# First weights in runs of 1, 1, 2 and 4 tiles, squares of the input placed after its splits and summed by VectorE, and seven products of zeros at the start

## The chip, the cores and the metric

The kernel runs on one core of a Trainium2 chip. The metric is the device time of one execution in microseconds (us), median of several runs; lower is better. Five engines share the work: TensorE (PE; its weight loads are listed as PEld), VectorE (DVE), ScalarE (ACT), GpSimd (POOL) and SyncE (SP), whose queue issues nearly all DMA transfers here.

## The reference, cut to what matters

The model is a two-layer trunk on 512 tokens with 16 meta tokens put in front (528 tokens, width 1024): a forgetting attention with 16 heads, a gated MLP with a causal convolution, an HGRN2 recurrence, and another gated MLP. Only the attention's beginning is touched by the change:

```python
def rms_norm(x, gain):
    x32 = x.astype(jnp.float32)
    y = x32 * lax.rsqrt(jnp.mean(x32 * x32, axis=-1, keepdims=True) + EPS)
    return (y * gain.astype(jnp.float32)).astype(x.dtype)

def fox_attention(h, norm_g, w_in, b_f, q_gain, k_gain, w_out):
    xn = rms_norm(h, norm_g)
    q, k, v, f_logit, o_gate = jnp.split(xn @ w_in, [D, 2 * D, 3 * D, 3 * D + H], axis=-1)
    q = rms_norm(q.reshape(B, L, H, hd), q_gain).astype(jnp.float32) * (hd ** -0.5)
    k = rms_norm(k.reshape(B, L, H, hd), k_gain).astype(jnp.float32)
    ...
    s = jnp.einsum('bqhd,bkhd->bhqk', q_blk, k) + c_blk[..., None] - c[:, :, None, :]
```

The mean of the squares over the 1024 features of a token is only needed as a factor per token, so projections can start on the unscaled input, and the factor can come later.

## The kernel before, in words

The input lies transposed: 8 blocks (`h[:, kt, :]`) of 128 features by 528 tokens. Every float32 product is made from three products of rounded parts: `normsplit` (L269) makes `xhi` on ScalarE (L273) and the remainder `xlo` on VectorE (L274) for each of the 8 blocks, and `weights` (L174) does the same with a weight tile: a DMA into `raw`, a cast `hi` on ScalarE, a subtraction `lo` on VectorE (L122). `proj_unit` (L196) then runs hi by hi (L204), hi by lo of the input (L207) and lo by hi of the input (L208) for each block, 24 products for one half of the tokens (264) and 128 output features.

Heads are worked in 8 pairs. A pair's q and k are projected (`stage_a`), for the first pair block by block in the order in which blocks arrive; the two result banks `p` are shared by all projections, and a bank comes free when ScalarE has read it twice: a square `sqq` (L486) and a scaled copy `rawq` or `rawk` (L487). A pair then goes through this chain:

- the squares are summed per head (L495), copied (`strow`) and carried by 4 DMAs (L500) into `am`; VectorE takes the inverse root in ten small steps (L284 to L288), giving `yr`; 2 DMAs (L510) carry it into `rows`;
- `stage_n`: four products with a selection matrix (L524, here called the spreading products) lay the factors over a bank `d`, one bank for all four; VectorE multiplies `rawq` and `rawk` by it (L525), and the result, split into `stg`, is carried by 6 DMAs (L551) into the slots `pk` of the pair's two heads; the forget terms `cneg` follow by DMA (L560);
- `stage_l`: per head six groups of scores (L666 to L669), maxima on VectorE (L679 to L687), exponentials with sums on ScalarE (L115), a logarithm, and then one small product (L700) that turns the result into rows, which DMAs (L705, L706) carry into the head's slot;
- `stage_t`: the scores once more with that row in (L722, L723) and the products with v (L737).

The mean of squares of the input itself is a chain of its own: `sumsq` (L259) squares each block on ScalarE (L263, L266) and adds it on GpSimd (L267); a product per token tile (L296) finishes the sum; its inverse root scales v and the gates, and through 4 DMAs (`et`, L375) it enters the `am` step of every pair.

The order within each engine is not written by hand. The code yields pieces of work that `weave` interleaves by cost, and a scheduler then places all instructions of the program by its own model of time. Each engine, and SP's queue, runs its list in order; an instruction whose operand is late holds up everything behind it on its engine. In the first microseconds SP issues vec (228 columns of vectors), the first q and k weights in two halves each, the 8 input blocks and the constants.

Of the kernel before, what the change touches and what calls it, by code (L numbers as in the profile page):

```python
# [24 lines left out]
T = 528  # L25
NM = 16
HF = 16
NPAIR = 8
NEARLY = 4
FF = 2816  # L30
NF = FF // P
EPS = 1e-6
# [48 lines left out]
class Builder:  # L81
# [42 lines left out]
    def setup(self):  # L124
        nc = self.nc
        cp = self.cp = self.pool("const")
        self.h = cp.tile([P, KT, T], F32, name="h")
        self.vec = cp.tile([P, V_END], F32, name="vec")
        nc.sync.dma_start(self.vec, self.a["vec"])
        self.wraw = self.pool("wraw", 2)  # L130
        self.whi = self.pool("whi", 3)
        self.wlo = self.pool("wlo", 3)
        q, k = (self.weights(self.a["wqk"][0, i], KT, parts=2) for i in range(2))
        order = [(q, 0), 0, (k, 0), 1, 2, 3, (q, 1), (k, 1), 4, 5, 6, 7]
        for x in order:
            if isinstance(x, int):
                nc.sync.dma_start(self.h[:, x, :], self.a["h0"][:, x, :])
            else:
                x[0][3][x[1]]()
        self.first = q[:3], k[:3]  # L140
        cst = cp.tile([P, C_END], F32, name="cst")
        self.cst = cst
        nc.sync.dma_start(cst, self.a["cst"])
        self.ident = cst[:, C_ID : C_ID + P]
        self.identr = cp.tile([P, P], F32R, name="identr")
        nc.vector.tensor_copy(self.identr, self.ident)
        self.xhi = cp.tile([P, KT, T], F32R, name="xhi")
        self.xlo = cp.tile([P, KT, T], F32R, name="xlo")
        self.x = [(self.xhi[:, k, :], self.xlo[:, k, :]) for k in range(KT)]
        self.rsb = cp.tile([P, T], F32, name="rsb")  # L150
        self.onesd = cp.tile([P, 2], F32, name="onesd")
        nc.vector.memset(self.onesd, 1.0 / D)
        self.tiny = self.pool("tiny", 2)
        self.sqp = self.pool("sqp", 2)
        self.ps = self.pool("ps", 1, PSUM)
        self.nbank = 0
        self.ss = None

    def anybank(self):
        self.nbank += 1  # L160
# [10 lines left out]
    def vcol(self, i):  # L171
        return self.vec[:, i : i + 1]

    def weights(self, src, n, w=P, parts=1):  # L174
# [12 lines left out]
        u = hi.rearrange("p (k c) -> p k c", c=w), lo.rearrange("p (k c) -> p k c", c=w), n  # L187
        if parts == 1:
            nc.sync.dma_start(raw, src)
            nc.scalar.copy(hi, raw)  # L190
            self.sub(lo, raw, hi.bitcast(F32))
            return u
        m = n * w // parts
        return *u, [partial(load, slice(i * m, i * m + m)) for i in range(parts)]

    def proj_unit(self, ps, units, x, t0, tn, prev=None):  # L196

# [58 lines left out]
                    yield 0.66  # L256
            put(t, ps[:tn, :256])

    def sumsq(self, kt, t0=0, eng=None, pool=None):  # L259
        nc = self.nc  # L260
        if kt == 0:
            self.ss = self.sqp.tile([P, T], F32, name="ss", tag="ss", bufs=1)
            nc.scalar.square(self.ss[:, t0:], self.h[:, kt, t0:])  # L263
        else:
            sq = (pool or self.sqp).tile([P, T], F32, name="sq", tag="sq" if pool is None else "rows")
            nc.scalar.square(sq[:, t0:], self.h[:, kt, t0:])  # L266
            self.ss_last = (eng or nc.vector).tensor_tensor(self.ss[:, t0:], self.ss[:, t0:], sq[:, t0:], ALU.add)  # L267

    def normsplit(self, gcol, t0=0):  # L269
        nc = self.nc  # L270
        for kt in range(KT):
            g = self.vcol(gcol + kt)
            nc.scalar.activation(self.xhi[:, kt, t0:], self.h[:, kt, t0:], AF.Copy, scale=g)  # L273
            nc.vector.scalar_tensor_tensor(  # L274
                self.xlo[:, kt, t0:], self.h[:, kt, t0:], g, self.xhi[:, kt, t0:].bitcast(F32), ALU.mult, ALU.subtract
            )
# [45 lines left out]
    def fox(self, ctx):  # L322
        nc, tc, a = self.nc, self.tc, self.a
# [3 lines left out]
        s2 = self.pool("fox2", 2, ctx=ctx)  # L327
# [1 line left out]
        gate = self.h  # L329
        self.normsplit(V_FOXN)  # L330
        for kt in range(KT):
            self.sumsq(kt, 0, nc.gpsimd, s2)
        lone = self.lone(sp, V_FOXN, T - 32)
        identb = sp.tile([P, P], BF16, name="identb")
        maskq = sp.tile([P, P], BF16, name="maskq")
# [29 lines left out]
        start = partial(self.bank, "s")  # L365
# [7 lines left out]
        for g in range(4):  # L373
            t0, tn = full[g % 2]
# [14 lines left out]
        z, e, w, u, lf = (sp.tile([P, CW], F32, name=n) for n in ("z", "e", "w", "u", "lf"))  # L389
# [218 lines left out]
        for p in range(-3, NPAIR):  # L608
# [26 lines left out]
            while gated and p >= max(gated[0], 5 + gated[0] // 4):  # L635
                m = gated.pop(0)
# [537 lines left out]
```

## Time and profile before

| what | value |
|---|---|
| time, median of 3 runs | 1498.43 us (1496.72 to 1500.53) |
| profiled execution, its own time | 1497.61 us |
| its span | 1495.8 us |
| PE busy | 1474.4 us (99%) |
| DVE, ACT, POOL busy | 892.8, 524.9, 32.3 us |
| mean granted TensorE clock | 0.998 |
| PE idle before the first product | 6.45 us |

The span is counted from the first instruction; the profiled execution's own time is 1.8 us longer than its span and 0.8 us below the median of the runs. In a row of the timeline the first number is the start, the second the duration, then engine, line, operation, operands and shapes; brackets give idle time before it and what ended it. A row that shows several instructions merged (x2, x4) gives the time from the first start to the last end. Line numbers such as L204 are those of the kernel before.

### The profile page before, as it was taken

How to read it: one execution, taken by the hardware profiler on the slowest of the kernel's cores; microseconds unless marked ns; L12 is line 12 of the kernel's file. 1: busy time of each engine (PE TensorE's matmuls, PEld its weight loads, DVE VectorE, ACT ScalarE, POOL GpSimd, SP SyncE). 2: the span in 40 equal slices, each digit the busy share in tenths (PEclk: the TensorE clock that was granted, in tenths of full speed). 3: DMA queues.
4: the chain of work that ended last, by engine and by line, in shares of the span. 5: the costliest groups of instructions: out<-in, count | busy, mean ns of one | idle time of the engine just before them, and what ended most of it. 6: DMA issues, size and time to landing. Idle time of an engine off the chain costs nothing.

```text
span 1495.8 us, 27540 instructions
## 1 busy us (share of the span) xinstructions
PE 1474.4 (99%) x11352; PEld 1361.8 (91%) x11352; DVE 892.8 (60%) x1881; ACT 524.9 (35%) x1007; POOL 32.3 (2%) x113
## 2 busy tenths in 40 slices
PE   7999999999999999999999999999999999999999
PEld 6888888979999999999999989999999989988887
DVE  6555555775677667643335667676566667675221
ACT  5456555654233222222222333333342232222121
POOL 6000000000000000000000000000000000000000
PEclk9999999999999999999999999999999999999999
DMA  4433344413232322322322211211132232332331
GB/s 156 117 103 88 102 106 127 116 52 96 96 99 85 96 88 88 95 78 80 104 83 71 72 35 52 71 63 52 57 101 97 86 99 87 96 98 83 121 104 60
DMA packets 44821, 133.33 MB, mean 89 GB/s; under 512 B 7432, under 2 KB 7944, under 8 KB 44696
## 3 DMA queue, kind: packets, MB, share of 16 engines
q1 hardware_dynamic: 44696, 131.57, 29.1%
q8 instruction: 89, 1.46, 0.4%
q14 instruction: 36, 0.29, 0.1%
HBM read 116.10 MB, written 2.10 MB: 79 GB/s over the span
## 4 chain that ended last, share of the span: by engine, by line
PE 96%; DMA 2%; DVE 1%; SPq 1%; ACT 1%; issue 0%; DVEq 0%; ACTq 0%
PE pss L208 13%; PE pss L207 13%; PE pss L204 13%; PE psp L204 12%; PE psp L207 12%; PE psp L208 12%; PE psp L253 5%; PE psc L737 2%; PE pss L888 1%; PE pss L666 1%; PE pss L722 1%; PE pss L867 1%; PE pss L723 1%; DMA h<-h 1%; PE pss L963 1%; PE pss L894 1%
## 5 line engine op out<-in xcount | busy, mean ns | idle before, releaser
L190 ACT CAST hi<-raw 128x1024 fp32r<-128x1024 f32 (+2 forms) x218 | 221.8, 1018 | 569.4 <-PE pss L207 235.3
L122 DVE TENSOR_TENSOR lo<-raw,hi 128x1024 fp32r<-128x1024 f32 (+2 forms) x222 | 262.8, 1185 | 148.7 <-ACT hi L190 143.5
L204 PE MATMUL psp<-xhi,hi 128*128 128x264 f32 (+2 forms) x1160 | 332.9, 288 | 6.5 <-ACT xhi L273 6.5
L207 PE MATMUL psp<-xlo,hi 128*128 128x264 f32 (+2 forms) x1160 | 333.6, 288 | 3.4 <-DVE xlo L274 3.4
L208 PE MATMUL psp<-xhi,lo 128*128 128x264 f32 (+2 forms) x1160 | 332.7, 287 | 0.0
L208 PE MATMUL pss<-xhi,lo 128*128 128x264 f32 (+2 forms) x824 | 253.7, 308 | 0.0
L207 PE MATMUL pss<-xlo,hi 128*128 128x264 f32 (+2 forms) x824 | 253.0, 307 | 0.0
L204 PE MATMUL pss<-xhi,hi 128*128 128x264 f32 (+2 forms) x824 | 252.9, 307 | 0.0
L204 PEld LDWEIGHTS psp<-xhi,hi 128*128 128x128 f32 x1160 | 219.1, 189 | 11.1 <-ACT xhi L273 6.5
L207 PEld LDWEIGHTS psp<-xlo,hi 128*128 128x128 f32 x1160 | 219.5, 189 | 7.7 <-DVE xlo L274 4.1
L208 PEld LDWEIGHTS psp<-xhi,lo 128*128 128x128 f32 x1160 | 219.5, 189 | 1.2 <-issue 1.0
L204 PEld LDWEIGHTS pss<-xhi,hi 128*128 128x128 f32 x824 | 155.2, 188 | 7.8
L207 PEld LDWEIGHTS pss<-xlo,hi 128*128 128x128 f32 x824 | 155.0, 188 | 7.9
L208 PEld LDWEIGHTS pss<-xhi,lo 128*128 128x128 f32 x824 | 155.0, 188 | 7.7
L207 PE MATMUL pss<-alo,hi 128*128 128x264 f32 (+1 forms) x330 | 106.1, 322 | 0.0
L208 PE MATMUL pss<-ahi,lo 128*128 128x264 f32 (+1 forms) x330 | 106.0, 321 | 0.0
L204 PE MATMUL pss<-ahi,hi 128*128 128x264 f32 (+1 forms) x330 | 105.9, 321 | 0.0
L115 ACT ACTIVATE s<-t 128x528 f32<-128x528 f32 (+1 forms) x44 | 28.1, 639 | 121.6 <-DVE t L1056 121.6
L253 PE MATMUL psp<-hi,xhi 128*128 128x256 f32 x232 | 67.4, 290 | 2.7 <-ACT v L540 2.7
L208 PEld LDWEIGHTS pss<-ahi,lo 128*128 128x128 f32 x330 | 62.3, 189 | 4.9
L204 PEld LDWEIGHTS pss<-ahi,hi 128*128 128x128 f32 x330 | 62.1, 188 | 4.9
L253 PE MATMUL psp<-lo,xhi 128*128 128x256 f32 x232 | 66.5, 287 | 0.0
(405 smaller groups left out, 2603.3 us busy)
## 6 DMA issues: line engine op xcount, KB each, us to landing
raw<-gu SPq DMA_DIRECT2D x88, 512.0 KB
raw<-dn SPq DMA_DIRECT2D x32, 448.0 KB
pk<-stg SPq DMA_DIRECT2D x48, 264.0 KB
raw<-dn SPq DMA_DIRECT2D x16, 512.0 KB
raw<-wqk SPq DMA_DIRECT2D x14, 512.0 KB
raw<-wv SPq DMA_DIRECT2D x8, 512.0 KB
raw<-wg SPq DMA_DIRECT2D x8, 512.0 KB
raw<-hv SPq DMA_DIRECT2D x8, 512.0 KB
```

Of the source, the lines that this page charges most:

```text
L115: ins = self.nc.scalar.activation(out, in_, func, **kw)
L122: self.nc.vector.tensor_tensor(out, x, y, ALU.subtract)
L190: nc.scalar.copy(hi, raw)
L204: ins = mm(ps, hi[:, i, :], xh, start=k == 0, stop=False)
L207: mm(ps, hi[:, i, :], xl, start=False, stop=False)
L208: mm(ps, lo[:, i, :], xh, start=False, stop=k == total - 1)
L253: mm(ps[:tn, :256], y[:, t0 : t0 + tn], w, start=n == 0, stop=n == 23)
L666: mm(o, q1[0:66, qs : qs + qn], k1[0:66, c0:c1], start=True, stop=False)
L722: self.score = mm(o, k1[0:98, ks : ks + kn], q1[0:98, q0:o1], start=True, stop=False)
L723: mm(o, k2[:, ks : ks + kn], q2[:, q0:o1], start=False, stop=True)
L737: ins = mm(o, v[:kn, j, 2 * (p % 2) + hd, :], w[hd][0], start=j == 0, stop=j == last)
L867: mm(pl[:, i, :, :], kp[:, t0 : t0 + tn], qk[:, t0 // 2 : (t0 + tn) // 2, :], start=True, stop=True)
```

## The change

Five edits in `setup`, `weights`, `sumsq`, `normsplit` and `fox`:

1. The first q and k weight tiles (8 column groups of 128 each) are loaded, cast and subtracted in runs of 1, 1, 2 and 4 groups instead of two runs of 4; the DMA order is interleaved anew with the input blocks, and `vec` is issued second instead of first.
2. `warm`: VectorE sets 128 by 512 bf16 zeros, and PE multiplies them seven times into bank `d`, which nobody reads.
3. The eight squares of the input may not be placed ahead of the last `xhi` (an ordering for the scheduler, not a wait).
4. The seven additions of squares move from GpSimd to VectorE.
5. The pools for PSUM banks and for squares are opened earlier, since `warm` uses both.

```diff
+NWARM = 7
...
-        nc.sync.dma_start(self.vec, self.a["vec"])
...
+        self.warm()
-        q, k = (self.weights(self.a["wqk"][0, i], KT, parts=2) for i in range(2))
-        order = [(q, 0), 0, (k, 0), 1, 2, 3, (q, 1), (k, 1), 4, 5, 6, 7]
+        q, k = (self.weights(self.a["wqk"][0, i], KT, parts=(1, 1, 2, 4)) for i in range(2))
+        order = [(q, 0), "vec", 0, (k, 0), (q, 1), 1, (k, 1), (q, 2), 2, (k, 2), 3, (q, 3), 4, (k, 3), 5, 6, 7]
         for x in order:
-            if isinstance(x, int):
+            if x == "vec":
+                nc.sync.dma_start(self.vec, self.a["vec"])
+            elif isinstance(x, int):
                 nc.sync.dma_start(self.h[:, x, :], self.a["h0"][:, x, :])
...
+    def warm(self):
+
+        nc = self.nc
+        z = self.sqp.tile([P, T], F32, name="zero", tag="sq")[:, :256].bitcast(BF16)
+        nc.vector.memset(z, 0.0)
+        o = self.bank("d")
+        for _ in range(NWARM):
+            nc.tensor.matmul(o, z[:, :P], z, start=True, stop=True)
...
-        m = n * w // parts
-        return *u, [partial(load, slice(i * m, i * m + m)) for i in range(parts)]
+        ends = [sum(parts[: i + 1]) * w for i in range(len(parts))]
+        return *u, [partial(load, slice(e - i * w, e)) for i, e in zip(parts, ends)]
...
-    def sumsq(self, kt, t0=0, eng=None, pool=None):
+    def sumsq(self, kt, t0=0, pool=None, prev=None):
         nc = self.nc
         if kt == 0:
             self.ss = self.sqp.tile([P, T], F32, name="ss", tag="ss", bufs=1)
-            nc.scalar.square(self.ss[:, t0:], self.h[:, kt, t0:])
+            ins = nc.scalar.square(self.ss[:, t0:], self.h[:, kt, t0:])
         else:
             sq = (pool or self.sqp).tile([P, T], F32, name="sq", tag="sq" if pool is None else "rows")
-            nc.scalar.square(sq[:, t0:], self.h[:, kt, t0:])
-            self.ss_last = (eng or nc.vector).tensor_tensor(self.ss[:, t0:], self.ss[:, t0:], sq[:, t0:], ALU.add)
+            ins = nc.scalar.square(sq[:, t0:], self.h[:, kt, t0:])
+            self.ss_last = nc.vector.tensor_tensor(self.ss[:, t0:], self.ss[:, t0:], sq[:, t0:], ALU.add)
+        if prev is not None:
+            self.after(ins, prev)
...
-            nc.scalar.activation(self.xhi[:, kt, t0:], self.h[:, kt, t0:], AF.Copy, scale=g)
+            self.split = nc.scalar.activation(self.xhi[:, kt, t0:], self.h[:, kt, t0:], AF.Copy, scale=g)
...
-            self.sumsq(kt, 0, nc.gpsimd, s2)
+            self.sumsq(kt, 0, s2, self.split)
```

The scheduler places the whole attention anew from this start on, so rows far behind the edits move too. Line numbers of the changed kernel run some 14 higher in the attention (L714 is the line that was L700, L736 was L722, L680 was L666, L538 was L524). Three places follow.

The first is ScalarE's list at the very start, before:

```order
2 L183 CAST hi<-raw 128x512
3 L273 ACTIVATE xhi<-h,vec 128x528
4 L263 ACTIVATE ss<-h 128x528
5 L183 CAST hi<-raw 128x512
6 L273 ACTIVATE xhi<-h,vec 128x528
7 L266 ACTIVATE sq<-h 128x528
8 L273 ACTIVATE xhi<-h,vec 128x528
```

and now, from the end of the splits:

```order
13 L195 CAST hi<-raw 128x512
14 L287 ACTIVATE xhi<-h,vec 128x528 x3
15 L275 ACTIVATE ss<-h 128x528
16 L278 ACTIVATE sq<-h 128x528 x2
17 L202 CAST hi<-raw 128x1024
18 L278 ACTIVATE sq<-h 128x528
19 L500 ACTIVATE sqq<-psp 128x264
20 L501 ACTIVATE rawq<-psp,qg 128x264
```

The squares left their places between the splits; all eight now stand behind the last `xhi`, some of them between the reads of the first pair's result banks.

The second is PE's list where the first head's L700 product stands (L714 in the changed kernel); `pk_265` and `pk_270` are the slots of heads 0 and 1. Before:

```order
496 L204 MATMUL psp<-xhi,hi 128x264
497 L207 MATMUL psp<-xlo,hi 128x264
498 L524 MATMUL psd<-rows_175,selr 128x264
499 L208 MATMUL psp<-xhi,lo 128x264
500 L204 MATMUL psp<-xhi,hi 128x264
501 L700 MATMUL pss<-identr,lr 10x128
502 L666 MATMUL pss<-pk_248 16x16
```

and now:

```order
503 L680 MATMUL pss<-pk_265 128x264
504 L681 MATMUL pss<-pk_265 128x264
505 L680 MATMUL pss<-pk_265 128x264
506 L681 MATMUL pss<-pk_265 128x264
507 L683 LDWEIGHTS identb
508 L683 MATMUL pss<-maskq,identb 128x128
509 L714 MATMUL pss<-identr,lr 10x128
510 L680 MATMUL pss<-pk_270 16x16
```

Before, 59 products (mostly projections) stood between head 0's last score product and this small product; now none does.

The third is PE's list at the last head's small product; slots 2 and 3 (`pk_253`, `pk_258` before, `pk_275`, `pk_280` now) hold the last pair. Before:

```order
2271 L700 MATMUL pss<-identr,lr 10x128
2272 L722 MATMUL pss<-pk_253 128x256
2273 L723 MATMUL pss<-pk_253 128x256
2274 L204 MATMUL psp<-pk_263,hi 128x264
2275 L207 MATMUL psp<-pk_268,hi 128x264
2276 L208 MATMUL psp<-pk_263,lo 128x264
```

and now:

```order
2292 L714 MATMUL pss<-identr,lr 10x128
2293 L736 MATMUL pss<-pk_275 128x256
2294 L737 MATMUL pss<-pk_275 128x256
2295 L736 MATMUL pss<-pk_280 128x256
2296 L737 MATMUL pss<-pk_280 128x256
2297 L216 MATMUL psp<-pk_285,hi 128x264
```

The last head's scores with its row (`pk_280`) now come 3 products behind the small product that the row is made from; before, they came 15 behind it, with 12 products of the output projection in between.

More of the change, by code (lines that the diff above doesn't have):

```diff
@@ L128, in setup @@
         self.vec = cp.tile([P, V_END], F32, name="vec")
-        nc.sync.dma_start(self.vec, self.a["vec"])
+        self.ps = self.pool("ps", 1, PSUM)
+        self.nbank = 0
+        self.sqp = self.pool("sqp", 2)
         self.wraw = self.pool("wraw", 2)
@@ L153, in setup @@
         self.tiny = self.pool("tiny", 2)
-        self.sqp = self.pool("sqp", 2)
-        self.ps = self.pool("ps", 1, PSUM)
-        self.nbank = 0
         self.ss = None
+    def warm(self):
[5 more added lines that the diff above has]
+            nc.tensor.matmul(o, z[:, :P], z, start=True, stop=True)
     def anybank(self):
@@ L172, in vcol, with weights @@
         return self.vec[:, i : i + 1]
-    def weights(self, src, n, w=P, parts=1):
+    def weights(self, src, n, w=P, parts=None):
         nc = self.nc
@@ L187, in weights @@
         u = hi.rearrange("p (k c) -> p k c", c=w), lo.rearrange("p (k c) -> p k c", c=w), n
-        if parts == 1:
+        if parts is None:
             nc.sync.dma_start(raw, src)
```

## The prediction, put on record before the changed kernel ran

> **What bounds the kernel now.** I read the page's busy times first, then the table of TensorE's waits, then the timeline of the opening.
>
> ```profile
> span 1495.8 us, 27540 instructions
> PE 1474.4 (99%) x11352; PEld 1361.8 (91%) x11352; DVE 892.8 (60%) x1881; ACT 524.9 (35%) x1007; POOL 32.3 (2%) x113
> ```
>
> TensorE is busy for all but 21.4 us, so only its waits, and stretches in which its products run slowly, can be won or lost. VectorE has 40% of its time free, ScalarE 65%.
>
> The largest waits, in total, times and longest:
>
> ```profile
> PE psp L204 <- ACT xhi L273: 6.5, 1, 6.5
> PE psp L207 <- DVE xlo L274: 3.4, 2, 2.7
> PE psp L253 <- ACT v L540: 2.7, 2, 1.4
> PE pss L722 <- DMA pk<-lrow: 1.9, 1, 1.9
> PE pss L666 <- DMA pk<-cneg: 1.2, 1, 1.2
> ```
>
> The first two are the opening. Its timeline:
>
> ```profile
> 5.67 0.74 ACT L273 ACTIVATE xhi<-h,vec 128x528 fp32r<-128x528 f32 x1 [0.16 <-DMA h<-h]
> ...
> 7.64 0.42 PE L208 MATMUL psp<-xhi,lo 128*128 128x264 f32 x1
> 7.87 0.42 PE L207 MATMUL psp<-xlo,hi 128*128 128x264 f32 x1
> 8.69 1.37 POOL L267 TENSOR_TENSOR ss<-ss,sq 128x528 f32<-128x528 f32 x1 [6.78 <-ACT sq L266]
> ...
> 11.41 0.28 PE L207 MATMUL psd<-xlo,hi 128*128 128x264 f32 x1
> 11.53 0.29 PE L208 MATMUL psd<-xhi,lo 128*128 128x264 f32 x1
> 15.77 1.81 DVE L274 SCALAR_TENSOR_TENSOR xlo<-h,vec,xhi 128x528 fp32r<-128x528 f32 x1
> 17.64 0.57 PE L207 MATMUL psp<-xlo,hi 128*128 128x264 f32 x1 [2.67 <-DVE xlo L274]
> 26.04 1.17 PE L296 MATMUL pss<-onesd,ss 128*128 128x2 f32 x10
> 28.18 0.39 PE L204 MATMUL psp<-xhi,hi 128*128 128x264 f32 x1
> ```
>
> Products follow each other at 0.23 us near 7.6 and at 0.12 from about 11. The first pair's 96 products (2 weights, 2 token halves, 24 each) would take 96 x 0.122 = 11.7 us; with the sum of squares after them they end only at 28.18. The opening thus loses 28.18 - 11.7 - 2.1 (for L296 and what follows it, 28.18 - 26.04) = 14.4 us: 6.5 ahead of the first product, half rate, the 2.67 on `xlo`, and what the next rows show. Their columns are the window, its length, then busy time with counts of PE, PEld, DVE, ACT and POOL, the granted clock, DMA share and GB/s.
>
> ```profile
> 18.00:21.00 3.00, 3.00 (x15) 3.00 (x15) 3.00 (x4) 1.25 (x2) 2.31 (x3) 0.50 0.28 107
> 21.00:26.00 5.00, 4.25 (x33) 3.95 (x32) 4.36 (x8) 1.58 (x3) 5.00 (x10) 0.99 0.04 7
> ```
>
> Right behind the wait of 2.67 us the clock fell to 0.50: 15 products in 3 us where some 25 would go.
>
> **The change: the opening.** Groups by shape give the price of each piece (after the bar: total us, mean ns):
>
> ```profile
> L274 DVE SCALAR_TENSOR_TENSOR xlo<-h,vec,xhi 128x528 fp32r<-128x528 f32 x16 | 12.2, 762 | 0.1
> L267 DVE TENSOR_TENSOR ss<-ss,sq 128x528 f32<-128x528 f32 x14 | 9.8, 701 | 0.1
> L266 ACT ACTIVATE sq<-h 128x528 f32<-128x528 f32 x21 | 13.3, 636 | 2.1 <-DVE h L1070 2.1
> L122 DVE TENSOR_TENSOR lo<-raw,hi 128x512 fp32r<-128x512 f32 x8 | 5.5, 683 | 0.8 <-ACT hi L190 0.7
> L190 ACT CAST hi<-raw 128x1024 fp32r<-128x1024 f32 x178 | 186.8, 1050 | 469.3 <-PE psp L207 207.9 <-PE pss L207 183.4 <-issue 37.1
> L486 ACT ACTIVATE sqq<-psp 128x264 f32<-128x264 f32 x30 | 11.7, 389 | 16.6 <-PE psp L208 16.5
> L487 ACT ACTIVATE rawq<-psp,qg 128x264 f32<-128x264 f32 x16 | 7.5, 478 | 1.3 <-DVE stg L122 1.3
> ```
>
> *Adds moved to VectorE.* 7 x 0.70 = 4.9 us of new VectorE work. VectorE's list has them behind the splits, and with 40% of it free they cost nothing by themselves. The gain is that GpSimd is quiet: the `xlo` at 15.77 took 1.81 us, the mean of 16 is 0.76, and the GpSimd addition itself ran 1.37 us. Without cover, that is with the adds ahead of the splits, it would be the 4.9 us.
>
> *Squares behind the splits.* ScalarE loses up to 8 x 0.64 = 5.1 us ahead of the last `xhi`. With both, VectorE's opening is 8 x 0.76 = 6.1 for `xlo`, some 3.4 for the `lo` of both weights (four 128x512 pieces were 4 x 0.68 = 2.7; smaller pieces add starts) and about 0.7 for two small subtractions: 10.2 us from about 5.6, when the first block is there, with a few tenths of waiting for data. The last `xlo` then comes near 16.4 instead of 17.6, and the products behind it end at 17.6, not 26.04, since there is no long wait and no half rate behind it; if the first products stay slow until about 10.7, as they do now, they end at 19.6.
>
> *What is late next.* The second pair's projections need the banks. In the list of the change, ScalarE has, behind the last `xhi`, three squares (3 x 0.64), a cast (1.05), and then `sqq` 0.39 and `rawq` 0.48; the third square needs a tile that the first VectorE add gives back. This frees the first bank between 19.2 and 20.2, whichever of the two ends above holds. The second pair so starts at about 20.1, and before it started at 28.18, 2.1 of which were the sum of squares, which is still to be paid (later, near 30 us, when its `ss` is complete at about 29; no wait). Gain: 26.0 - 20.1 = **-6.0 us**, between -4 (the bank at 22, if ScalarE waits for data) and -8 (the bank at 18).
>
> *Smaller runs of weights and the zeros.* The same bytes are loaded; the first cast is of 128 columns instead of 512, and the first product still waits for the first `xhi`, now with one DMA issue fewer ahead of its weights and `vec` behind it. I take the start as unchanged within 0.5 us. Seven products of 256 columns at a slow spacing take 7 x 0.43 (the duration near 7.6 us) = 3.0 us in otherwise idle time. If they raise the clock, the first projections end up to 2 us earlier, but the bank above hides that: 0, at most -0.3.
>
> The Trainium skill, "TensorE: Matmul & The Clock Gate", Part 1 on the clock gate, says that full rate comes after some 3.4 us of sustained work and that the gate falls back after at least one whole idle window of that length. By that rule the 3.0 us of zeros would be just too short, and a 2.67 us wait should not have dropped the clock; the granted 0.50 behind it says that it did, and the measurement decides. By the rule the waits below would cost only themselves, and the time would be the forecast; by the row they could cost more, which is the second rival.
>
> **The change: the attention behind it.** The lists show that the middle and the end of the attention are ordered anew. The first place is the chain from the first pair's spreading products to the second's:
>
> ```profile
> 56.11 0.28 PE L524 MATMUL psd<-rows,selr 128*128 128x264 f32 x1
> 57.55 6.11 SPq L551 DMA_DIRECT2D pk<-stg  x6
> 63.76 3.72 SPq L500 DMA_DIRECT2D am<-strow  x4
> 70.43 1.44 SPq L560 DMA_DIRECT2D pk<-cneg  x2
> 71.41 0.18 DVE L122 TENSOR_TENSOR yr<-rqq,yr 64x33 fp32r<-64x33 f32 x1
> 71.96 1.42 SPq L510 DMA_DIRECT2D rows<-yr  x2
> 75.14 0.28 PE L524 MATMUL psd<-rows,selr 128*128 128x264 f32 x1
> ...
> 84.29 0.29 PE L524 MATMUL psd<-rows,selr 128*128 128x264 f32 x1
> 87.25 6.16 SPq L551 DMA_DIRECT2D pk<-stg  x6
> ```
>
> From 56.11 to 75.14 are 19.0 us: SP's six transfers of packs, four of `am`, VectorE's root at 71.41, two of rows, and 1.8 until the rows have landed (73.38 to 75.14). Between the two spreading products TensorE's list had 142 products, 120 now. In before they filled 19.0 - 1.22 = 17.8 us (1.22 is the wait on `cneg` in the table), 0.125 each; 120 fill 15.0 us. So 19.0 - 15.0 = **+4.0 us** of waiting. It contains the second place of the order, where head 0's small product now stands right behind the scores. What it waits for took, for the next head:
>
> ```profile
> 90.98 0.43 DVE L685 TENSOR_REDUCE negm<-pss 128x1 f32<-128x264 f32 x1 [1.44 <-PE pss L667]
> 94.12 0.17 DVE L122 TENSOR_TENSOR lr<-ls,lr 128x5 fp32r<-128x5 f32 x1
> ```
>
> 94.29 - 90.98 = 3.3 us with nothing on TensorE in between, which is the lower bound. The upper is 6.7: SP's list has ten `cneg` transfers (1.44 / 2 = 0.72 each) ahead of the two of rows, where it had two next to them, and some of these may hold the rows up by 2.7.
>
> Then three spreading products follow each other with nothing between, on the one bank `d`; each needs VectorE's multiplication of the last (0.43 on average, L525 below, and starts on both sides), about 0.9 less its own time: **+1.6** (0.6 to 2.0).
>
> ```profile
> L525 DVE TENSOR_TENSOR rawq<-rawq,psd 128x264 f32<-128x264 f32 x16 | 6.8, 426 | 18.1 <-PE psd L524 18.0
> ```
>
> The third piece is the second pair's first score. In the timeline it took 84.29 to 87.25 until the packs were issued, 3.1 for the three of the first head (half of 6.16) and 1.8 to land: 7.8 us. TensorE's list had 81 products there, 32 now, 3.9 us at 0.122: **+3.4 to 3.8**, I take 3.4, since some of the packs' issue may move up. Against it stand the waits of before in this stretch that find no place in the new order, on `v` (1.41) and on `cneg` (1.22): **-2.6**.
>
> At the end, the third place:
>
> ```profile
> 333.06 0.22 PE L700 MATMUL pss<-identr,lr 128*10 128x128 f32 x1
> 336.88 0.36 PE L722 MATMUL pss<-pk 98*128 98x256 f32 x1 [1.86 <-DMA pk<-lrow]
> ```
>
> The row took 3.8 us from the small product to the scores, 1.86 of it waited. With 3 products in between instead of 15, 12 x 0.12 = 1.45 less is covered: **+1.4** (0 to 1.5). The gated MLPs and the recurrence keep their order.
>
> Sum: -6.0 + 4.0 + 1.6 + 3.4 - 2.6 + 1.4 = **+1.8 us**. Against the profiled execution's own 1497.6 that is 1499.4; the median of the runs is 0.8 higher, which would make 1500.2, but that is far inside the runs' own spread of 3.8. I keep **1499.4**, no change: 0.3% of 1498.4 is 4.5 us, about what a measurement of this kernel can tell from nothing, so the bounds of "same" are 1493.9 and 1502.9.
>
> **The rivals.** *The lead survives.* If in the new kernel SP is less loaded in the 19.0 us chain (six packs that start earlier, the root found ready), the chain shrinks below the 15.0 us of products, and only the small product's 3.3 us are left, with 0.6 for the spreading products and the next score's packs in time: -6.0 + 3.3 + 0.6 - 2.6 = -4.7, so 1492.9, and faster. For it: a new order was made around the new start, and of the 19.0 us some 3 are SP issuing `am` behind packs. Against: SP's ten `cneg`.
>
> *Waits drop the clock.* After a 2.67 us wait the clock was 0.50 for 3.4 us here, which is 1.7 us lost. Three waits of 3.3 us or more are new, in a place where there were only short ones. Place: TensorE behind the second pair's spreading products; price: 1.7 each for two of them, and 1.2 for rows behind part of the `cneg`: 1.8 + 3.4 + 1.2 = +6.4, so 1504, slower. It decides from two drops on. Against: the waits are broken by short products, and the drop in before came with products already sparse.
>
> *The change does not do what it says*: the zeros do not lift the clock, or the small runs do not bring the first product forward. By the bank this moves the end by 0.3 at most: 1499.7, inside the forecast.
>
> **How the numbers follow.** The forecast of no change, with the third rival in it, has 0.52; the surviving lead 0.26; the dropped clock 0.22. The likeliest case's own range is 1494 to 1503. All low ends together (-8, 3.3, 0.6, 0, -2.6, 0) give -6.7, all high ones (-4, 6.7, 2.0, 3.8, -2.6, 1.5, and 3.4 for the clock) +10.8; neither is likely whole, so the range is 1492.0 to 1505.0. Faster 0.26, same 0.52, slower 0.22.
>
> **What would show it.** Right: no `xlo` above 0.9 us in the opening, no granted 0.50 near 18 us, the second pair's first product at 19 to 21 us; a wait of about 4 us in total ahead of a spreading product or of the small product near 70 us, one of 3 to 4 us on packs some ten us later, 2 to 3.5 us on the last head's row. It would be wrong if the second pair still starts after 24 us, if TensorE's idle time beyond 30 us is under 5 us in the attention, or if the granted clock falls behind those waits. The forecast would also fall if the second pair begins early but a projection behind it waits for weights.

## The result, and the profile after

The changed kernel takes 1509.08 us (median of 4 runs, 1508.54 to 1510.49) against 1498.37 us of the kernel before on the same chip: ratio 1.0072, 95% interval 1.0055 to 1.0090. It is slower by some 10.7 us, where 1499.4 in a range up to 1505.0 was predicted. The profiled execution took 1510.49 us, 12.9 more than that of before; the accounts below are made against these two, so they explain 12.9 and not the 10.7 of the medians.

The page of the changed kernel:

```profile
span 1508.7 us, 27551 instructions
PE 1484.4 (98%) x11359; PEld 1366.2 (91%) x11359; DVE 888.2 (59%) x1893; ACT 527.6 (35%) x1011; POOL 21.4 (1%) x106
```

Its table of TensorE's waits (L714 was L700, L736 was L722, L680 was L666, L538 was L524):

```profile
PE pss L714 <- DVE lr L123: 3.9, 1, 3.9
PE pss L736 <- DMA pk<-lrow: 3.4, 1, 3.4
PE pss L680 <- DMA pk<-cneg: 2.8, 1, 2.8
PE psd L538 <- DMA rows<-yr: 2.6, 2, 2.0
```

The two waits of the opening are gone from the top, and four of the attention stand there. The windows by stage show where it happened; columns as in the prediction. The kernel before:

```profile
0.00:30.00 30.00, 20.12 (x127) 18.57 (x128) 21.27 (x37) 17.87 (x30) 20.54 (x35) 0.94 0.58 192
30.00:200.00 170.00, 165.52 (x1317) 143.08 (x1316) 92.17 (x304) 84.46 (x246) 5.55 (x24) 1.00 0.39 103
200.00:300.00 100.00, 100.00 (x787) 87.29 (x787) 64.98 (x190) 58.48 (x165) 1.16 (x10) 1.00 0.42 109
300.00:400.00 100.00, 96.56 (x759) 89.16 (x757) 63.37 (x149) 47.80 (x107) 0.37 (x4) 0.98 0.26 84
```

The changed kernel:

```profile
0.00:30.00 30.00, 27.20 (x183) 23.64 (x184) 19.31 (x44) 21.68 (x41) 13.48 (x35) 1.00 0.59 194
30.00:200.00 170.00, 160.64 (x1234) 137.01 (x1233) 87.22 (x298) 81.27 (x237) 1.76 (x16) 0.95 0.38 98
200.00:300.00 100.00, 96.63 (x738) 82.93 (x739) 59.59 (x184) 54.16 (x155) 1.08 (x10) 0.98 0.39 102
300.00:400.00 100.00, 95.17 (x734) 87.06 (x733) 64.99 (x148) 51.16 (x117) 0.23 (x2) 0.97 0.31 90
```

Idle is the length less PE's busy time. "Slow" is busy time by what the granted clock lacks to 1.00, added up over windows of 1 to 50 us inside each stage. In the first 10 us that column shows 1.00 although the products stand 0.22 us apart; this half rate, about 2.2 us of slow work in both kernels, is left out on both sides. The zeros (3.2 us) count as lost.

| stage, us | before: idle + slow | changed: idle + slow (+ zeros) | difference |
|---|---|---|---|
| 0 to 30, opening | 9.9 + 1.5 | 2.8 + 0 + 3.2 | -5.4 |
| 30 to 200, first pairs | 4.5 + 0 | 9.4 + 5.9 | +10.8 |
| 200 to 300 | 0 + 0 | 3.4 + 1.7 | +5.1 |
| 300 to 400, end of the attention | 3.4 + 1.6 | 4.8 + 3.1 | +2.9 |

The sum is +13.4. From the first product of the first gated MLP to the last product of the program both take about the same (1103.8 and 1103.4 us), so all of it lies in the attention. For these two kernels the account closes (the first MLP starts 13.0 us later); for three of the kernels below, those with the third edit alone, with their own buffer, and with that order mended, it gives 3.5 to 4 us more than the start of the MLP shows, and the reason stays open. Shares of a few microseconds are therefore rough.

The opening of the changed kernel:

```profile
5.34 0.81 PE L216 MATMUL psp<-xhi,hi 128*128 128x264 f32 x2 [0.98 <-ACT xhi L287]
9.46 0.42 PE L219 MATMUL psp<-xlo,hi 128*128 128x264 f32 x1
9.86 0.28 PE L219 MATMUL psc<-xlo,hi 128*128 128x264 f32 x1
16.88 0.76 DVE L288 SCALAR_TENSOR_TENSOR xlo<-h,vec,xhi 128x528 fp32r<-128x528 f32 x1
20.36 0.39 PE L216 MATMUL psp<-xhi,hi 128*128 128x264 f32 x1
30.66 1.17 PE L310 MATMUL pss<-onesd,ss 128*128 128x2 f32 x10
```

The last `xlo` takes 0.76 us and comes at 16.9, the second pair starts at 20.36 as forecast, but the sum of squares (L310) comes at 30.66, where it came at 26.04. What hangs on it, in the order of time:

```profile
32.92 2.87 SPq L389 DMA_DIRECT2D et<-ssr  x4
36.95 0.38 ACT L510 COPY strow<-psd 128x264 f32<-128x264 f32 x1 [1.74 <-DMA et<-ssr]
41.12 0.19 DVE L517 TENSOR_TENSOR am<-am,et 64x33 f32<-64x33 f32 x1 [0.57 <-DMA am<-strow]
64.05 5.96 SPq L565 DMA_DIRECT2D pk<-stg  x6
74.03 7.49 SPq L574 DMA_DIRECT2D pk<-cneg  x10
76.64 0.17 PE L680 MATMUL pss<-pk 66*16 66x16 f32 x1 [2.81 <-DMA pk<-cneg]
83.30 0.27 PE L714 MATMUL pss<-identr,lr 128*10 128x128 f32 x1 [3.87 <-DVE lr L123]
```

Before, the same two early rows were:

```profile
32.62 0.38 ACT L496 COPY strow<-psd 128x264 f32<-128x264 f32 x1 [1.74 <-PE psd L495]
36.80 0.19 DVE L503 TENSOR_TENSOR am<-am,et 64x33 f32<-64x33 f32 x1 [0.74 <-DMA am<-strow]
```

Everything behind the sum of squares is 4 to 6.5 us later than before (packs 64.05, before 57.55), while the projections of the second pair start 7.8 us earlier (5.7 in work, since before the sum of squares stood ahead of them). The projections are what covers this chain, and they have been used up: head 0's first score and its small product now stand 17 products apart in TensorE's list, before 94. The waits then take the clock with them; windows of the changed kernel:

```profile
78.00:81.00 3.00, 1.43 (x8) 1.11 (x6) 3.00 (x10) 1.50 (x6) 0.00 (x0) 0.51 0.03 6
84.00:87.00 3.00, 3.00 (x14) 2.54 (x14) 1.73 (x5) 1.41 (x6) 0.00 (x0) 0.50 0.02 6
90.00:93.00 3.00, 2.48 (x15) 1.55 (x15) 1.73 (x7) 1.84 (x5) 0.21 (x2) 0.50 0.05 10
93.00:96.00 3.00, 3.00 (x19) 2.97 (x19) 0.24 (x1) 0.00 (x0) 0.00 (x0) 0.64 0.93 197
```

It stays at half from 78 to 95 us. Two more places follow later, a later pair's rows and the last head's row:

```profile
214.14 0.39 PE L538 MATMUL psd<-rows,selr 128*128 128x264 f32 x1 [1.98 <-DMA rows<-yr]
...
348.33 0.55 PE L736 MATMUL pss<-pk 98*128 98x256 f32 x1 [3.36 <-DMA pk<-lrow]
```

### The profile page after: what moved, and what is told of

It reads as the page before. It is cut to its first block, busy times and chain, and to the rows that moved or that the text cites. A ratio compares the mean times of both kernels' runs of the same rounds, so it can differ in the third digit from the quotient of the medians.

```text
span 1508.7 us, 27551 instructions
## 1 busy us (share of the span) xinstructions
PE 1484.4 (98%) x11359; PEld 1366.2 (91%) x11359; DVE 888.2 (59%) x1893; ACT 527.6 (35%) x1011; POOL 21.4 (1%) x106
## 4 chain that ended last, share of the span: by engine, by line
PE 93%; SPq 3%; DMA 2%; DVE 1%; ACT 1%; issue 1%; DVEq 0%; ACTq 0%
PE pss L219 13%; PE pss L220 13%; PE pss L216 13%; PE psp L216 12%; PE psp L219 12%; PE psp L220 11%; PE psp L265 6%; PE psc L751 2%; PE pss L902 1%; SPq L565 1%; PE pss L680 1%; PE pss L881 1%; SPq L514 1%; PE pss L736 1%; PE pss L737 1%; PE pss L977 1%
## 5 line engine op out<-in xcount | busy, mean ns | idle before, releaser
L123 DVE TENSOR_TENSOR lo<-raw,hi 128x1024 fp32r<-128x1024 f32 (+4 forms) x226 | 261.2, 1157 | 152.3 <-ACT hi L202 146.5
L219 PEld LDWEIGHTS pss<-alo,hi 128*128 128x128 f32 x330 | 62.1, 188 | 5.0
```

What stands on the lines that cost most here:

```text
L123: self.nc.vector.tensor_tensor(out, x, y, ALU.subtract)
L219: mm(ps, hi[:, i, :], xl, start=False, stop=False)
```

## The experiments

**First group: the parts, the zeros and the clock.** The third edit was suspected at once: it puts the squares behind the splits, and the sum of squares with them. One run takes it back, one makes it alone. The kernels with one edit alone are made from the changed one by taking the others back; the earlier opening of the pools (the fifth edit) stays in them. Each ratio is to the kernel before on the same chip, whose medians were 1497.6 to 1498.4 us; differences to the changed kernel are taken across sessions. Where an experiment must not be ordered anew by the scheduler, its kernel carries a table with each engine's order of the attention and ties each instruction to the one ahead of it, so that its lists are those of the kernel that it copies, row by row.

The change without its third edit:

```diff
-            self.sumsq(kt, 0, s2, self.split)
+            self.sumsq(kt, 0, s2)
```

> The change without its third edit: the squares may stand between the splits again; all else as changed. Late-sum theory: the loss comes from the sum of squares, which stands at the head of the normalisation of every pair and which the third edit makes late (its first product at 30.7 us in the changed kernel, 26.0 before). Here that product runs at 23 to 26 us, the first pair's packs are issued at 57 us or earlier instead of 64, no wait in the attention is over 2.7 us, the granted clock stays at 1.0 between 70 and 100 us, and the time is 1491 to 1496, at least 12 us under the changed kernel. Rival, lead that cannot be kept: whatever starts the projections earlier uses up the cover of the chain through SP; then waits of 5 us or more in sum stay between 60 and 100 us, and the time is 1500 to 1507.

1498.92 us, ratio to before 1.0007 (0.9998 to 1.0015). Ten of the eleven lost microseconds are back, and 93 products stand again between the first score and the small product. The sum of squares starts at 23.9 us. But neither number was met: there is no gain. The wait is still there, and so is the half clock behind it, if shorter; from the table of waits, and a window:

```profile
PE pss L680 <- DMA pk<-cneg: 3.7, 1, 3.7
```

```profile
72.00:74.00 2.00, 2.00 (x11) 1.76 (x10) 0.74 (x3) 1.74 (x7) 0.00 (x0) 0.50 0.06 10
```

The first score comes at 71.8 us, 1.2 earlier than before, though the projections are 5 us ahead in work (second pair at 20.98, where before 28.18 included 2.1 for the sum of squares): here the forget terms, which VectorE finishes at 66.0, are what arrives last, and the lead runs out in front of them. The rival was right in that, and wrong in the size.

The third edit alone, on the kernel before:

```diff
-            self.sumsq(kt, 0, nc.gpsimd, s2)
+            self.sumsq(kt, 0, nc.gpsimd, s2, self.split)
```

> Before with the third edit alone: squares behind the splits, adds still on GpSimd, weights in two halves, no zeros. Late-sum theory: first product of the sum of squares at 29 us or later, waits of 6 us or more and a half clock around 75 to 95 us as in the changed kernel, 8 to 16 us over before (1506 to 1514). Rival, only the edits together do it: within 3 us of before (1495 to 1502).

1503.52 us, ratio 1.0035 (1.0023 to 1.0048). The first score and the small product stand 19 products apart, and am+et comes at 39.35 us instead of 36.80. Half of the loss of the whole change, less than expected. By the account above, the stage from 30 to 200 us lost as much as in the changed kernel (10.5 us idle and 6.9 slow, there 9.4 and 5.9); what is missing here is the loss near 214 us. The largest waits of the attention are those of the chain:

```profile
PE psd L537 <- DMA rows<-yr: 4.2, 2, 2.5
PE pss L735 <- DMA pk<-lrow: 3.4, 1, 3.4
```

The zeros, with the order of the changed kernel held fixed:

```diff
-NWARM = 7
+NWARM = 0
```

> The changed kernel in exactly its order on every engine (held by an order table for the attention), without the seven products of zeros. Zeros-do-nothing: the products of the opening stay at the 0.22 us spacing until 9.5 to 10.5 us as in the changed kernel, and the time is within 1 us of it (1508 to 1510). Rival, zeros shorten the slow start: half rate lasts 1.5 us or more longer, and the second pair starts 0.5 to 2 us later.

1506.94 us, ratio to before 1.0064 (1.0050 to 1.0077), under the 1508 to 1510 expected, and a little under the changed kernel, if anything. The products of the opening change their spacing at the same place without the zeros (starts 0.22 us apart up to the first row, 0.12 from the second; in this kernel all products have one line, that of the table's helper):

```profile
9.32 0.42 PE L107 MATMUL psp<-xhi,lo 128*128 128x264 f32 x1
...
9.72 0.28 PE L107 MATMUL psp<-xhi,lo 128*128 128x264 f32 x1
```

With the zeros it was 9.46 and 9.86. There they did nothing.

The clock by itself. Same order, and products that nobody reads in the two longest waits of the middle (`fill` issues so many products of 264 columns into the bank that the waiting product will overwrite):

```diff
+            if fill and i == 0:
+                self.fill(fill[0], ps, q2[:, :P], k2[:, :264])   # 24, head 0's first score
...
+        if fill:
+            self.fill(fill[1], pr, q2[:, :P], k2[:, :264])       # 32, its small product
```

> The changed kernel in exactly its order, with products that nobody reads put into its two longest waits in the middle: 24 ahead of head 0's first score, 32 ahead of its small product; the waited-for work is untouched. Clock theory: half of the loss in the middle is the granted clock, 0.5 from 78 to 95 us, in which TensorE was busy some 12 us for work of 6. With the gaps filled the clock stays at 1.0 and the time falls by 5 to 9 us (1500 to 1504). Rival, the waits themselves: the chain paces TensorE, the clock only makes work slow that had time, and the time stays within 2 us of the changed kernel (1507 to 1511).

1506.37 us, ratio 1.0055 (1.0041 to 1.0068): 2.7 us under the changed kernel, between the two expectations. The clock held through the filled waits and fell behind them, at the spreading products, which were not filled:

```profile
81.00:84.00 3.00, 2.86 (x24) 2.27 (x23) 1.83 (x9) 1.00 (x6) 0.22 (x2) 1.00 0.06 10
...
87.00:90.00 3.00, 2.20 (x13) 1.06 (x14) 2.04 (x7) 2.26 (x7) 0.21 (x2) 0.50 0.00 0
```

By the same account as above, slow work from 30 to 200 us went from 5.9 to 3.0 us, and 2.7 us of the median came back. One for one is not shown by this: the profiled execution is 2.5 us above the median of its runs and lost 1.9 us more to the clock at the end of the attention. Runs of one and the same kernel price the clock better. Among the 35 of the kernel before that were timed beside the next four experiments, the five shortest (mean granted clock 0.998 to 0.999) lie 5.1 us below the five longest (0.994 to 0.996), where the clock accounts for some 5.7. So slow microseconds are mostly real ones; but the fillers take 56 x 0.12 = 6.7 us in place of the waits, and most of the loss stays. The waits come first.

**Second group: the chain itself.** The trace names a second delay in the chain: `strow` waits for the transfers of `ssr` (36.95, above), since both use one buffer. Giving `ssr` another one shortens the chain without touching the third edit:

```diff
-        ssr = s2.tile([2, T], F32, name="ssr", tag="strow", bufs=1)
+        ssr = s2.tile([2, T], F32, name="ssr", tag="rows")
```

> The changed kernel with one edit: the row of the sum of squares on its way to `et` gets another buffer, so that the first pair's `strow` no longer has to wait for the `et` transfers that read it (in the changed kernel Q's products end at 27.0 us and the copy waits until 36.95; am+et is at 41.1). The third edit stays, the sum is as late as before. Late-chain theory: am+et comes at 37 to 38 us, the first pair's packs 3 to 6 us earlier than 64.05, the order of the attention has its cover back (60 products between head 0's first score and its small product instead of 17), and the time falls by 8 to 14 us, to 1495 to 1501. Rival, the sum of squares itself must come earlier: little moves, over 1504.

1494.88 us, ratio to before 0.9979 (0.9971 to 0.9988): 14.2 us under the changed kernel, and 3.5 under the kernel before. 61 products stand between first score and small product; first score at 67.9 us (76.64 in the changed kernel); am+et comes a little earlier than expected, and the largest wait that is left stands at the spreading products:

```profile
36.53 0.19 DVE L517 TENSOR_TENSOR am<-am,et 64x33 f32<-64x33 f32 x1
...
79.70 0.39 PE L538 MATMUL psd<-rows,selr 128*128 128x264 f32 x1 [3.57 <-DVE rawk L539]
81.87 1.11 PE L509 MATMUL psd<-sqq,hsel 128*32 128x264 f32 x8 [1.78 <-DVE rawk L539]
```

The sum of squares still comes at 30.2 us. It need not be earlier; what follows it had to be.

The same buffer without the third edit:

> The change without its third edit and with the same other buffer. Late-chain theory: am+et at about 32 us instead of 35.5, first score 2 to 4 us earlier than 71.8, the wait on cneg and the half clock behind it gone or under 2 us, 1493 to 1496. Rival, a lead that the chain through SP cannot keep: the first score within 1 us of 71.8 and the time within 1.5 us of 1498.9.

1498.09 us, ratio 0.9999 (0.9990 to 1.0008): the rival. am+et came 1.3 us earlier only (34.18), and the first score at 71.6 waited 3.4 us for `cneg` as before. The chain of the rows was not what came last there.

The same buffer in the kernel before, in exactly its order:

> The kernel before with the other buffer alone; every engine's order is the same as before, row by row. am+et at 34.5 to 35.5 us instead of 36.8. Both theories: the chain has cover in the order of before, so no more than its small waits (1.2 on cneg, 1.4 on v) can go: 1495 to 1498.5.

1498.12 us, ratio 0.9997 (0.9987 to 1.0007), as expected: no gain where the chain has its cover. One row of the timeline is worth keeping with the window behind it: a wait of only 1.23 us, among the small products of the scores, was followed by half clock:

```profile
71.94 0.17 PE L666 MATMUL pss<-pk 66*16 66x16 f32 x1 [1.23 <-DMA pk<-cneg]
```

```profile
74.00:76.00 2.00, 2.00 (x11) 2.00 (x11) 0.70 (x2) 1.00 (x4) 0.00 (x0) 0.50 0.06 14
```

The fourth edit alone, the additions on VectorE:

```diff
-            self.sumsq(kt, 0, nc.gpsimd, s2)
+            self.sumsq(kt, 0, nc.vector, s2)
```

> Before with the fourth edit alone, the seven additions on VectorE. Opening: no xlo over 0.9 us, the wait of 2.67 us and the half clock behind it gone, the sum of squares' first product at 21 to 23.5 us instead of 26.0. Late-chain theory: the whole chain comes 2.5 to 4.5 us earlier and the projections with it, so the lead is kept in the middle; the end waits 1.5 us longer on the last row as in the changed kernel: 1494.5 to 1497.5. Rival, lead that cannot be kept: 1498 to 1501.

1495.54 us, ratio 0.9986 (0.9977 to 0.9994). `xlo` stays at 0.76 us, the sum of squares starts at 21.1 us and am+et is at 33.1. Here projections and chain come earlier together, and 2.8 us stay, in spite of 3.4 us of waiting on the last head's row. Of the three edits that were made alone (the first, third and fourth), it is the only one that gains.

**Third group: order or latency, and a better kernel.** The buffer changed the chain and, through the scheduler, the order. The changed kernel's order, held fixed, with the new buffer:

> The changed kernel's order on every engine, held by an order table, with the other buffer for the row of the sum of squares. It tells what the buffer gives by itself from what the new order of the last-but-one group of runs gave. The row's wait goes, but the `am` transfers still stand behind `et` on SP: am+et at 39 to 40 us instead of 41.1. Order theory (the loss of the changed kernel lies in how its lists stand: 17 products between first score and small product, three spreading products in a row): 1505 to 1508.5, at most 4 us better. Latency theory (the late transfers alone): 1495 to 1500.

1507.54 us, ratio 1.0065 (1.0051 to 1.0079). The row's wait is shorter (am+et at 39.89), the small product waits nearly as long as before (3.52 us, 3.87 in the changed kernel):

```profile
39.89 0.18 DVE L107 TENSOR_TENSOR am<-am,et 64x33 f32<-64x33 f32 x1
...
83.19 0.27 PE L107 MATMUL pss<-identr,lr 128*10 128x128 f32 x1 [3.52 <-DVE lr L107]
```

So of the 14.2 us, some 1.5 are the transfer, which is no more than the runs spread, and some 12.7 the order. The new order with the shared buffer was not run, so the two are split from one side only. By the lists, the late chain does its harm through the scheduler: it plans the scores late, fills the time ahead with the projections, and nothing is left to lay between them; the scheduler's own times stand in no trace.

The order that the buffer gave, with one place mended by hand (VectorE's multiplications of `rawk`, and the steps to the small product, ahead of two subtractions on weights that arrive at 76.9 us). ScalarE's casts of these weights went back likewise. VectorE's list, shortened, as it was and as it is:

```
rawq, lo, ls, rawk, lo, lr, stg, rawk, lr, stg, lrow
rawq, ls, lr, lr, rawk, stg, rawk, stg, lrow, (3 maxima), lo, ..., lo
```

> The changed kernel with the other buffer, in the order that this gave, and in that order one place mended by hand: VectorE's two multiplications of rawk, and ScalarE's and VectorE's steps to the small product, ahead of a cast and a subtraction of weights that arrive late (at 76.9 us; behind them TensorE waited 3.6 and 1.8 us at spreading products, and ran at half clock from 82.8 on). Theory: these 5.4 us shrink to 1 to 2 and the half clock goes with them: 3 to 6 us under the kernel without the mending, 1489 to 1492.5. Rival, the stall moves on to SP's next transfers: 1493 to 1496.

1490.99 us, ratio to before 0.9956 (0.9943 to 0.9968): 3.9 us under the run without the mending, 7.1 under the kernel before, the fastest of all. One stretch of half clock was expected to go and stayed (79.0 to 82.4 us). The rows that waited 3.57 and 1.78 us:

```profile
77.05 0.39 PE L107 MATMUL psd<-rows,selr 128*128 128x264 f32 x1 [0.52 <-DVE rawk L107]
78.01 0.65 PE L107 MATMUL psd<-sqq,hsel 128*32 128x264 f32 x8 [0.57 <-DVE rawk L107]
```

The same with `NWARM = 12`:

> The kernel of the run before with 12 products of zeros instead of 7, 5.2 us at their spacing of 0.43, to 6.3 us; the first splits are there at 5.3. If sustained work of 4.5 us lifts the clock, as it did behind the first real products, it rises at 4.6 to 6 us, the first real products run at 0.12, and the first pair's end comes up to 2 us earlier; the time is within 1 us of the run before, since the chain of the sum of squares is not touched. Rival, products of zeros do not count as work for the clock: slow spacing until 10 us or later, 0.5 to 1.5 us slower.

1491.99 us, ratio 0.9961 (0.9948 to 0.9973): within 1 us, as expected. The 12 zeros took 4.53 us, not 5.2, since the clock rose in their midst (their starts are 0.43 us apart up to 4.6 us and 0.22 from 4.9 on), and the first real products ran at 0.12 from 5.8 us on. But in the run before, with 7 zeros, it had risen too:

```profile
5.35 0.51 PE L107 MATMUL psp<-xhi,hi 128*128 128x264 f32 x2 [1.17 <-ACT xhi L107]
5.70 0.29 PE L107 MATMUL psc<-xhi,hi 128*128 128x264 f32 x1
```

Products of zeros do count as work, then: in no kernel without them did the products run at 0.12 before 9.5 us. Whether seven are enough differs from one profiled execution to the next (slow until 9.7 us in the changed kernel, 0.12 by 5.7 here, in nearly the same opening), and the end of the program does not feel it.

The first edit alone, the weights in smaller runs:

```diff
-        q, k = (self.weights(self.a["wqk"][0, i], KT, parts=2) for i in range(2))
+        q, k = (self.weights(self.a["wqk"][0, i], KT, parts=(1, 1, 2, 4)) for i in range(2))
```

> Before with the first edit alone, weights in runs of 1, 1, 2 and 4. First product at 5.3 to 5.5 us instead of 6.45; GpSimd still adds, so xlo of 1.4 to 1.8 us and a wait of 1 to 3 us on the last ones stay; the sum of squares stays where it was, 25 to 26 us. Late-chain theory: an earlier projection alone gives nothing, 1496 to 1500. Rival: the 1.1 us of the start stay to the end and more, 1493 to 1496.

1497.35 us, ratio 0.9999 (0.9991 to 1.0008). First product at 5.46 us, `xlo` still up to 1.80 us, nothing gained: an earlier projection alone is worth nothing. (The run also has the change's new order of the first transfers.)

The main marks of these traces in us (start of the row named; the count of products is from TensorE's list, where the trace shows some products as two):

| kernel | sum of squares | am+et | first score | products to the small one | first MLP | time |
|---|---|---|---|---|---|---|
| before | 26.0 | 36.8 | 73.0 | 94 | 388.0 | 1498.4 |
| changed | 30.7 | 41.1 | 76.6 | 17 | 401.1 | 1509.1 |
| third edit alone | 28.6 | 39.4 | 74.0 | 19 | 394.3 | 1503.5 |
| all but the third | 23.9 | 35.5 | 71.8 | 93 | 390.3 | 1498.9 |
| fourth alone | 21.1 | 33.1 | 70.0 | 93 | 385.8 | 1495.5 |
| changed, own buffer | 30.2 | 36.5 | 67.9 | 61 | 385.7 | 1494.9 |
| its order mended | 30.5 | 36.8 | 68.3 | 61 | 381.6 | 1491.0 |

The two kernels with few products between first score and small product are the slow ones.

## Why the prediction was wrong

*The opening was right.* -6.0 was forecast, -5.4 measured, with the bank as the limit (second pair at 20.36, forecast 20.1), quiet `xlo` of 0.76, and zeros without effect on the time. The words "no wait" for the late sum of squares were the flaw: TensorE did not wait at L310, but the whole chain behind it did. The new order was in hand when the sum was made, and its waits were priced; what was not seen is why the order came out so. The prediction saw that the sum is complete later and looked only at the product that reads it, not at `et`, `strow` and `am`, which come after. That is the cause the runs name: undoing the third edit returns 10 of the 11 us, making it alone costs 5 to 6, and shortening the chain behind it by other means returns 14.

*The waits of the middle were in the right places, but shared out otherwise.* Waiting rose by 9.4 - 4.5 = +4.9 us where the terms gave 4.0 + 1.6 + 3.4 - 2.6 = +6.4. `cneg` and the small product took 2.8 + 3.9 = 6.7, the upper bound and not the 4.0 chosen: the ten `cneg` transfers, which were weighed for the rows behind them, were late themselves. The wait on `v` fell from 2.7 to 1.0 us, where the term of -2.6 had counted on 1.4 of it and on the wait for `cneg`, which grew. The spreading products gave 3 x 0.5 = 1.6, as forecast. The second pair's first score waited 0.4 us, not 3.4, because the products ahead of it took 6.3 us instead of 3.9, 15 of them at half clock, and so covered most of the transfer. That the sum of these terms came out near is in part luck: one was 2.7 us too low and another 3.0 too high. The end waited 1.4 us more, which is the term.

*The step that failed most is the clock.* The sum held nothing for it; the second rival had 1.7 us for each of two drops, 3.4 us at half rate each. Behind the opening the sum had 7.8 us, all of it waiting; 18.8 were measured there, 9.7 waiting and 9.1 slow (5.9 in the middle, 1.7 near 214 us, 1.5 at the end). So of the 11.0 us that the sum lacks, 9.1 are the clock. That the clock falls behind those waits is one of the signs by which the prediction itself said it would be wrong. One drop lasted 17 us, because the score products and the spreading products behind the wait were short and broken by further waits of 0.5 us; the clock came back only behind 3.5 us of dense projections (they start at 91.7, and the spacing is 0.12 from 95.1 on). The rival named the right mechanism at less than half its price: it took each drop for one stretch of 3.4 us, and this one was five.

*A place was left out.* Only the first two pairs and the end were followed in the lists. The wait of 1.98 us on rows at 214 us, 1.4 us of smaller ones near it and 1.7 us of slow work add 5.1.

*The range* therefore ended 4 us too low. All high ends together gave +10.8, and the profiled execution shows +12.9: what went past its bound is the clock, and the place that had no term.

*The first rival*, a lead that survives, was true of another kernel, that with the additional buffer: there it ended at -3.5, near the -4.7 worked out for it. The nearness is luck: the waits of 3.57 and 1.78 us there are not those of the rival.

## What to carry to other kernels

When a change starts one stream of work earlier and delays another, follow the delayed one to the first place where the main engine needs it, not to the first instruction that reads it; work that runs ahead is cover spent. Where a scheduler orders the program by its own model of time, count in the new lists how many products stand between the start of a latency chain and the product that ends it, over the whole stage and not only at its head: 94 and 61 were good here, 17 and 19 were not. A high number is not enough: with 93 and a wait of 3.7 us ahead of the first score, nothing was gained. A wait in a place where products are small costs more than its length, because the clock stayed low here until dense work had filled some 3.4 us; and a buffer shared by two links of a chain can cost more than the memory it saves.

## What the runs showed of the hardware that was not expected

The granted clock does not go by the longest gap. It fell behind waits of 2.67 us (before) and 2.81 us (changed), and behind one of 1.23 us in the kernel before with the other buffer (rows above). It did not fall behind one of 1.60 us at the same place in the kernel with the fourth edit alone:

```profile
72.00:74.00 2.00, 1.86 (x17) 1.68 (x15) 2.00 (x4) 1.84 (x9) 0.00 (x0) 1.00 0.04 8
```

Nor did it fall behind the wait of 1.22 us at the same product in the kernel before, whose lists are row by row those of the kernel with 1.23. As far as these traces show, what decides is how busy TensorE is in a window of 3.41 us, and not a single wait. In every one of these traces the time between two changes of the clock is a whole multiple of 3.41 us (the 17 us above are five). Laid on that grid, the window with the wait of 1.22 us and the one with 1.23 are these:

```profile
72.30:75.72 3.42, 2.67 (x21) 2.38 (x22) 2.88 (x6) 3.06 (x12) 0.00 (x0) 1.00 0.05 7
```

```profile
70.21:73.62 3.41, 2.18 (x18) 1.67 (x17) 2.31 (x6) 3.09 (x9) 0.00 (x0) 1.00 0.12 35
```

TensorE was busy for 78% of the first and for 64% of the second; behind the second came half clock, from 73.6 to 77.0 us. Over the fourteen traces, up to 1450 us, the clock fell behind 35 of the 37 windows with full clock that were busy for up to 58%, and behind none that was busy for more than 64%; once down, it came back only behind windows that were busy for 95% or more. The same wait can so be free or dear, by where it falls on the grid.

The Trainium skill ("TensorE: Matmul & The Clock Gate", Part 1: The HAM clock gate) has a free-running window of about 3.4 us, one whole idle one of which brings the clock down. The length agrees with the 3.41 us; the rows with 1.23 and 2.67 us speak against a window that is idle as a whole. That nearly the same opening had its clock raised before 5.7 us in one kernel and at 9.7 in another, by the spacing of the products, agrees with a window that does not start with the kernel.

VectorE's `xlo` took 1.81 us beside GpSimd's additions and 0.77 beside GpSimd's memsets, which fill the same stretch in the changed kernel; the second row is the window around it, whose fifth busy time is GpSimd's:

```profile
7.34 0.77 DVE L288 SCALAR_TENSOR_TENSOR xlo<-h,vec,xhi 128x528 fp32r<-128x528 f32 x1 [0.85 <-ACT xhi L287]
```

```profile
6.00:12.00 6.00, 5.48 (x31) 5.26 (x31) 2.99 (x8) 2.81 (x6) 5.67 (x12) 1.00 0.84 273
```

The Trainium skill ("SBUF — State Buffer", "Who interferes with whom") has it that an operation with two inputs in SBUF contends with a GpSimd instruction that reads SBUF and not with one that only writes; the traces agree.
